# From the output projection on: three engines in source order, the squares of the norm later, FFN sums in accumulators

## The chip, the core and the metric

The kernel runs on one core of one Trainium2 chip. The metric is device time in microseconds (us) for one execution. TensorE multiplies matrices into PSUM banks, VectorE and ScalarE work on tiles in SBUF and read PSUM, GpSimd works on SBUF alone, and SyncE's queue issues nearly all transfers. In the rows PE is TensorE's matmuls, PEld its weight loads, DVE VectorE, ACT ScalarE, POOL GpSimd and SP (SPq) SyncE's queue.

## The reference

One layer of a streaming encoder. Two token branches are merged, projected and added to the residual `h`; then comes a feed-forward network and a last norm:

```
def _merge_ffn(h, ya, yb, ga, gb, w_out, norm_ffn, w_up, w_down):
    m = jax.nn.sigmoid(ga) * ya + jax.nn.sigmoid(gb) * yb
    h = h + jnp.einsum('btd,de->bte', m, w_out)
    u = jnp.einsum('btd,df->btf', _rmsnorm(h, norm_ffn), w_up)
    return h + jnp.einsum('btf,fd->btd', jnp.square(jax.nn.relu(u)), w_down)
```

`w_out` is 1024 x 1024, `w_up` 1024 x 4096, `w_down` 4096 x 1024, all float32. There are 544 columns of tokens (16 meta tokens with padding, 32 of a running stream, 512 of the prompt). Since relu squared of a scaled row is the scale squared times relu squared, the FFN is computed on unnormed `h`, and the norm's factor r2 = 1/(mean of h squared + eps) is multiplied in after the down projection.

## The kernel before, in words

Every float32 matrix is split in two: a rounded high part, made by ScalarE (`split_hi`, a copy), and the remainder, made by VectorE (`split_lo`, a subtraction). A product is three matmuls: high x high, low x high, high x low. All weights are loaded by SyncE into three slots (tag `raw`, 512 KB each), split, and kept in two slots (`whi`, `wlo`).

The stages of interest, in order:

- **Output projection** ("wo"), eight units of 48 matmuls in the order `WO_ORDER`. `evac_o` (VectorE) adds the result into `xr`, which becomes `hs[d]`, the residual. `operands(d)` then makes of two such tiles, d and d + 4, the seven combined operands (B11, BM, B21, B22, BT4, BN, BT3) that the next stage multiplies, each split in `hh` and `hl`. GpSimd squares `hs[d]` and sums the squares into `sqa`.
- Four **chunks** (`ch`), each an up stage and a down stage. The **up stage** has four pairs (`up_pair`); a pair is a Strassen-like scheme of seven products of 12 matmuls: first a11 and s1, then s2, s4, s3, a12, a22. They go into three PSUM banks, X, V and Y. The first, third, fifth and seventh product all add into X, and between them ScalarE copies X out (L1327, L1333, L1340, L1350), so that each of these products must wait for the copy that comes before it. Then relu squared (L1345, L1351; VectorE), `uh` (ScalarE) and `ul` (VectorE), first for two of four quarters, then for the other two.
- The **down stage** has eight units d of 48 matmuls; VectorE multiplies each result by r2 into `dt` (L1396), and GpSimd (VectorE in the last chunk) adds it to `hs[d]` (L1398). In the last chunk transposes, the last norm and the output follow in between (`final_part`, `final_norm`).

Weights of a pair are prepared in steps by the generator `pair_prep`: s31 (two sums at once, L280), s24 (L285, L288), and the splits. Its four loads fill two `raw` tiles: u2 (a21 and a12) and u1 (a11 and a22). The steps of pair p + 1 are written between the products of pair p: `pre(1)` runs one step of the generator that was started last. `use(key)` finishes a unit's steps and starts the loads of the next one. u2's slot comes free with the split of a12, u1's with that of a22.

What sets the order: the kernel's text is not the order in which engines run it. A planner goes through all instructions when the kernel is built, with costs of its own, and gives each engine its instructions in the order in which it finds them ready. Each engine then works down its list, waiting on semaphores. So in the trace before, steps of `pair_prep` stand earlier or later than in the text, as it fitted.

Of the kernel before, what the change touches and what calls it, by code (L numbers as in the profile page):

```python
# [8 lines left out]
F32 = mybir.dt.float32  # L9
# [6 lines left out]
P = 128  # L16
# [31 lines left out]
def tile_hybrid_step(  # L48
# [13 lines left out]
    tpool = ctx.enter_context(tc.tile_pool(name="tpool", bufs=1))  # L62

# [192 lines left out]
    def pair_prep(n, key, parts):  # L256
# [920 lines left out]


# [7 lines left out]
    sqa = pairw["R"].tile([P, TM], F32, name="sqa")  # L1186
# [7 lines left out]
    def operands(d):  # L1194
        j, g = d % 4, gffn[:, d: d + 1]
        H_, L_ = hH[j], hL[j]

        def split(i, src):
            n = src.shape[1]
            split_hi(H_[:, i: i + n, :], src)  # L1200
            split_lo(L_[:, i: i + n, :], src, H_[:, i: i + n, :])

        if d < 4:
            bt = bts[0] = pairw["R"].tile([P, 3, HT], F32, tag="bt", name=f"bt{j}")
            ACT.activation(bt[:, 0:3:2, :], halves(hs[d]), AF.Copy, scale=g)
            DVE.tensor_tensor(bt[:, 1, :], bt[:, 0, :], bt[:, 2, :], ALU.subtract)
            split(B11, bt[:, 0:2, :])
# [7 lines left out]
        split(BN, bt[:, 1:3, :])
        split(B21, b2)
        DVE.scalar_tensor_tensor(bt[:, 0, :], bt[:, 1, :], -1.0, b2[:, 0, :], ALU.mult, ALU.subtract)
        split(BT4, bt[:, 0:1, :])

    bts = [None]  # L1220
    for n, d in enumerate(WO_ORDER):
# [3 lines left out]
        if n == KD - 1:  # L1225
            pre(3)
# [21 lines left out]
    pre(3)  # L1248

# [68 lines left out]
    def up_pair(ch, j):  # L1318
# [4 lines left out]
        u = fpool.tile([P, 4, HT], F32, tag="u", name=f"u{ch}_{j}", bufs=2)  # L1323
# [17 lines left out]
        DVE.tensor_tensor(u[:, 3, :], x3, u[:, 3, :], ALU.add)  # L1341
        pre(1)
        product(Y, W["a12"], B21, True)
        DVE.tensor_tensor(u[:, 0, :], yv, u[:, 0, :], ALU.add)
        DVE.scalar_tensor_tensor(u[:, 0:2, :], u[:, 0:2, :], 0.0, u[:, 0:2, :], ALU.max, ALU.mult)  # L1345
        split_hi(uh[:, 0:2, :], u[:, 0:2, :])
        split_lo(ul[:, 0:2, :], u[:, 0:2, :], uh[:, 0:2, :])
        pre(1)
        product(X, W["a22"], BT4, False)
        ACT.activation(u[:, 2, :], xv, AF.Copy)  # L1350
        DVE.scalar_tensor_tensor(u[:, 2:4, :], u[:, 2:4, :], 0.0, u[:, 2:4, :], ALU.min, ALU.mult)  # L1351
        split_hi(uh[:, 2:4, :], u[:, 2:4, :])
        split_lo(ul[:, 2:4, :], u[:, 2:4, :], uh[:, 2:4, :])
        pre(1)
# [6 lines left out]
    for ch in range(NCH):  # L1361
        uh, ul = [], []
        for j in range(4):
            h_, l_ = up_pair(ch, j)
            uh.append(h_)
            ul.append(l_)
            if ch == 0 and j == 1:
                for a, b in OC:
                    ps = psany(f"ps_r2_{a}")
                    mm(ps[:, : b - a], ones_d, sqa[:, a:b], True, True)  # L1370
                    DVE.tensor_scalar(r2[:, a:b], ps[:, : b - a], EPS, None, ALU.add)
                    DVE.reciprocal(r2[:, a:b], r2[:, a:b])
        last_ch = ch == NCH - 1
        for d in range(KD):
# [13 lines left out]
            for ci, part in (((0, 0), (1, 0), (0, 1), (1, 1)) if d == 0 else ((0, 0), (0, 1), (1, 0), (1, 1))):  # L1388
# [52 lines left out]
```

## Time and profile before

| | us |
|---|---|
| median of the runs | 837.34 |
| lowest run | 835.44 |
| the profiled execution, its own time | 835.72 |
| span of its trace | 834.0 |
| TensorE matmuls busy | 805.4 (97%) |
| VectorE busy | 561.7 (67%) |
| ScalarE busy | 355.6 (43%) |
| GpSimd busy | 192.3 (23%) |

The mean granted clock of TensorE was 0.989 of full speed. A busy share is a mean over all stages; the stages have different limits, so it is the rows by stage that tell what sets the time. In a timeline row the last bracket gives how long the engine had sat idle and what released it.

### The profile page before, as it was taken

To read this page: it belongs to the slowest core of one execution; us is meant where nothing else is said; L and a number is where in the kernel's file an instruction comes from. 1 tells how busy PE (TensorE), PEld (TensorE's weight loads), DVE (VectorE), ACT (ScalarE), POOL (GpSimd) and SP (SyncE) were. 2 spreads that over 40 slices of the span, in tenths; PEclk is the share of its full clock that TensorE was granted. 3 is DMA by queue.
4 is the path that set the end of the run, shared out by engine and by line. 5 is a ranking of instruction groups with operands and counts; after the bars stand their busy time and mean duration, and the time that the engine had idled before them with its cause. 6 is when DMAs were issued, how large, how long until landed. Compare 5 with 4: busy or idle time off the path is not lost.

```text
span 834.0 us, 15007 instructions
## 1 busy us (share of the span) xinstructions
PE 805.4 (97%) x6087; PEld 771.7 (93%) x6087; DVE 561.7 (67%) x1020; ACT 355.6 (43%) x663; POOL 192.3 (23%) x194
## 2 busy tenths in 40 slices
PE   8998999999999999999997999999999999999995
PEld 6877898898999999999996999999999999999995
DVE  5866258798768464467679893689438873688554
ACT  6761454555445632322444641246214551255223
POOL 4315112211121384015445002210122002300000
PEclk8999999999999999999998999999999999999999
DMA  8523223431521123232223342332332332414202
GB/s 246 153 59 90 51 54 94 124 78 51 134 80 51 51 76 103 76 101 77 85 68 102 84 119 76 85 94 79 104 97 77 101 102 85 118 52 129 75 26 108
DMA packets 133303, 75.38 MB, mean 90 GB/s; under 512 B 14545, under 2 KB 128513, under 8 KB 133233
## 3 DMA queue, kind: packets, MB, share of 16 engines
q1 hardware_dynamic: 132192, 72.27, 30.8%
q0 software_dynamic: 1024, 2.14, 1.1%
q8 instruction: 48, 0.79, 0.4%
q14 instruction: 23, 0.18, 0.1%
q10 hardware_dynamic: 16, 0.00, 0.0%
HBM read 69.57 MB, written 4.83 MB: 89 GB/s over the span
## 4 chain that ended last, share of the span: by engine, by line
PE 67%; DVE 15%; DMA 7%; ACT 5%; POOL 3%; issue 3%; SPq 0%; ACTq 0%; POOLq 0%; DVEq 0%
PE ps_dn L117 23%; PE ps_gb L117 5%; PE ps_ga L117 5%; PE ps_x L117 5%; DMA wr<-in_w_up_dram 4%; PE ps_fv L117 3%; PE ps_ya L117 3%; PE ps_yb L117 3%; PE ps_fk L117 2%; PE ps_v L117 2%; PE ps_wo L117 2%; DVE wlo L123 2%; DVE wl L123 2%; PE ps_y L117 2%; DMA wr<-in_w_in_dram 2%
## 5 line engine op out<-in xcount | busy, mean ns | idle before, releaser
L120 ACT ACTIVATE wh<-wr 128x1024 fp32r<-128x1024 f32 x78 | 82.4, 1057 | 184.4 <-PE ps_dn L117 82.7
L123 DVE TENSOR_TENSOR wl<-wr,wh 128x1024 fp32r<-128x1024 f32 x78 | 113.5, 1456 | 31.3 <-ACT wh L120 30.8
L1398 POOL TENSOR_TENSOR xres<-xres,dt 128x288 f32<-128x288 f32 (+1 forms) x48 | 41.2, 864 | 235.1 <-DVE dt L1396 235.1
L245 POOL TENSOR_TENSOR wr<-wr,gmix 128x1024 f32<-128x1024 f32 x30 | 58.1, 1938 | 144.8 <-DMA wr<-in_w_in_dram 111.2
L117 PE MATMUL ps_dn<-uh,wl 128*128 128x256 f32 (+1 forms) x512 | 85.6, 288 | 0.0
L117 PE MATMUL ps_dn<-ul,wh 128*128 128x256 f32 (+1 forms) x512 | 85.2, 288 | 0.0
L117 PE MATMUL ps_dn<-uh,wh 128*128 128x256 f32 (+1 forms) x512 | 85.0, 288 | 0.0
L117 PEld LDWEIGHTS ps_dn<-ul,wh 128*128 128x128 f32 x512 | 72.6, 189 | 0.0
L117 PEld LDWEIGHTS ps_dn<-uh,wl 128*128 128x128 f32 x512 | 72.5, 188 | 0.0
L117 PEld LDWEIGHTS ps_dn<-uh,wh 128*128 128x128 f32 x512 | 72.3, 188 | 0.0
L1396 DVE TENSOR_TENSOR dt<-ps_dn,fin 128x288 f32<-128x288 f32 x64 | 28.0, 439 | 65.5 <-PE ps_dn L117 65.3
L120 ACT ACTIVATE whi<-s 128x512 fp32r<-128x512 f32 (+1 forms) x32 | 27.0, 842 | 37.7 <-issue 14.4
L117 PE MATMUL ps_x<-hh,whi 128*128 128x272 f32 x128 | 37.9, 296 | 3.6 <-ACT hh L120 1.9
L117 PE MATMUL ps_x<-hh,wlo 128*128 128x272 f32 x128 | 37.8, 295 | 1.0 <-DVE wlo L123 0.9
L117 PE MATMUL ps_x<-hl,whi 128*128 128x272 f32 x128 | 37.5, 293 | 0.6 <-DVE hl L123 0.6
L117 PE MATMUL ps_v<-hh,whi 128*128 128x272 f32 x128 | 37.8, 296 | 0.1
L117 PE MATMUL ps_v<-hl,whi 128*128 128x272 f32 x128 | 37.5, 293 | 0.0
L117 PE MATMUL ps_v<-hh,wlo 128*128 128x272 f32 x128 | 37.3, 292 | 0.0
L123 DVE TENSOR_TENSOR wlo<-s,whi 128x512 fp32r<-128x512 f32 (+1 forms) x32 | 33.9, 1060 | 4.7 <-ACT whi L120 4.7
L907 ACT ACTIVATE sb<-sb,m 128x144 f32<-128x144 f32 (+3 forms) x32 | 18.3, 573 | 36.3 <-DVE m L902 36.3
L280 DVE TENSOR_TENSOR s<-wr,wr 128x1024 f32<-128x1024 f32 x16 | 20.0, 1252 | 16.7 <-DMA wr<-in_w_up_dram 16.7
L120 ACT ACTIVATE uh<-u 128x544 fp32r<-128x544 f32 x32 | 21.0, 658 | 21.9 <-DVE u L1351 11.2
(463 smaller groups left out, 2231.3 us busy)
## 6 DMA issues: line engine op xcount, KB each, us to landing
wr<-in_w_up_dram SPq DMA_DIRECT2D x64, 256.0 KB, 3.4
wr<-in_w_down_dram SPq DMA_DIRECT2D x32, 512.0 KB, 4.1
wr<-in_w_in_dram SPq DMA_DIRECT2D x30, 512.0 KB, 3.9
wr<-in_w_out_dram SPq DMA_DIRECT2D x8, 512.0 KB, 3.9
cb<-cPd SPq DMA_DIRECT2D x8, 264.0 KB, 3.9
x_t<-in_x_prompt_dram SPq DMA_DIRECT2D x4, 512.0 KB, 5.4
gvraw<-in_w_in_dram SPq DMA_DIRECT2D x4, 512.0 KB, 8.2
fvraw<-in_w_in_dram SPq DMA_DIRECT2D x4, 512.0 KB, 3.9
```

What stands on the lines that cost most here:

```text
L117: return TE.matmul(out, lhsT, rhs, start=start, stop=stop, skip_group_check=True)
L120: ACT.activation(out, in_, AF.Copy)
L123: (eng or DVE).tensor_tensor(out, in_, hi.bitcast(F32), ALU.subtract)
L245: POOL.tensor_tensor(raw, raw, gmix.unsqueeze(2).to_broadcast([P, KD, P]), ALU.mult)
L280: DVE.tensor_tensor(s31, u1, u2[:, 0:1].to_broadcast([P, 2, k4, P]), ALU.add)
L907: exps.append(ACT.activation(sb, sb, AF.Exp, bias=m, scale=-1.0, accum_out=rs).ins)
L1396: DVE.tensor_tensor(dt_[:, : b - a], ps[:, : b - a], r2[:, a:b], ALU.mult)
L1398: (DVE if last_ch else POOL).tensor_tensor(hs[d][:, a:b], hs[d][:, a:b], dt_[:, : b - a], ALU.add)
```

## The change

Three things change. First, from the line where the output projection begins, TensorE, ScalarE and VectorE no longer get a planned order: they take their instructions in the order of the source. GpSimd and SyncE stay planned. The source is rearranged along with it: steps of `pair_prep` and of `operands` are reordered, a step stands ahead of the copy that follows a product, and the seven quarters' tiles become pairs of halves (`half_pair`). Second, the squares of `hs[d]` and their sum move from the output projection to the down stage of chunk 0, and r2 to the first unit of chunk 1's down stage. Third, the down results of chunks 0 to 2 are gathered unscaled in `acc[d]` (ScalarE copies in chunk 0, VectorE adds in chunks 1 and 2); after chunk 2 VectorE multiplies by r2 and adds to `hs[d]`. GpSimd's 48 additions are gone.

```
+    vpool = ctx.enter_context(tc.tile_pool(name="vpool", bufs=1))
...
         if key[0] == "dn":
-            yield
+            for _ in range(4 if key[2] == 0 else 1):
+                yield
...
         s31 = t(pairw["R"], "s31", 2, F32)
         DVE.tensor_tensor(s31, u1, u2[:, 0:1].to_broadcast([P, 2, k4, P]), ALU.add)
-        A = t(wpool, "whi", bufs=2), t(wpool, "wlo", bufs=2)
-        split(A, 0, ["a11"], u1[:, 0:1])
         yield
         s24 = t(pairw["R"], "s24", 2, F32)
         DVE.tensor_tensor(s24[:, 0], s31[:, 1], u1[:, 0], ALU.add)
+        yield
+        A = t(wpool, "whi", bufs=2), t(wpool, "wlo", bufs=2)
+        split(A, 0, ["a11"], u1[:, 0:1])
+        DVE.tensor_tensor(s24[:, 1], s24[:, 0], u2[:, 1], ALU.add)
+        yield
         split(A, 1, ["s1"], s31[:, 1:2])
         yield
-        DVE.tensor_tensor(s24[:, 1], s24[:, 0], u2[:, 1], ALU.add)
         B = t(wpool, "whi", bufs=2), t(wpool, "wlo", bufs=2)
-        yield
         split(B, 0, ["s2", "s4"], s24)
         yield
...
+        for nm, src in (("s3", s31[:, 0:1]), ("a12", u2[:, 1:2]), ("a22", u1[:, 1:2])):
+            split((t(pairw["L"], nm + "h", 1), t(pairw["L"], nm + "l", 1)), 0, [nm], src)
+            yield
...
+    ordered = ctx.enter_context(tc.manual_schedule(
+        engines={mybir.EngineType.PE, mybir.EngineType.Activation, mybir.EngineType.DVE}))
...
+    def operands(d, mid=None):
...
         ACT.activation(b2, halves(hs[d]), AF.Copy, scale=g)
+        DVE.scalar_tensor_tensor(bb[:, 0, :], ba[:, 1, :], -1.0, b2[:, 1, :], ALU.mult, ALU.subtract)
+        DVE.tensor_tensor(bb[:, 1, :], b2[:, 1, :], bb[:, 1, :], ALU.subtract)
+        if mid:
+            mid()
+        hi(BN, bb)
+        hi(B21, b2)
+        DVE.scalar_tensor_tensor(ba[:, 0, :], bb[:, 0, :], -1.0, b2[:, 0, :], ALU.mult, ALU.subtract)
+        lo(BN, bb)
+        hi(BT4, ba[:, 0:1, :])
+        lo(B21, b2)
+        lo(BT4, ba[:, 0:1, :])
...
         if n == KD - 1:
-            pre(3)
+            pre(4)
...
-            POOL.tensor_tensor(sqa, xr, xr, ALU.mult)
-            POOL.tensor_tensor(sq, xr, xr, ALU.mult)
-            POOL.tensor_tensor(sqa, sqa, sq, ALU.add)
+        operands(d, (lambda: pre(1)) if n == KD - 1 else None)
...
     def up_pair(ch, j):
...
         product(X, W["a11"], B11, True)
+        pre(1)
+        ACT.activation(fa[:, 0, :], xv, AF.Copy)
         product(V, W["s1"], BM, True)
+        pre(1)
+        ACT.activation(fb[:, 1, :], vv, AF.Copy)
         product(X, W["s2"], BN, False)
+        pre(1)
+        ACT.activation(fa[:, 1, :], xv, AF.Copy)
         product(V, W["s4"], B22, False)
+        pre(1)
+        DVE.tensor_tensor(fa[:, 1, :], vv, fa[:, 1, :], ALU.add)
         product(X, W["s3"], BT3, False)
+        pre(1)
         x3 = fpool.tile([P, HT], F32, tag="x3", name=f"x3_{ch}_{j}", bufs=2)
         ACT.activation(x3, xv, AF.Copy)
+        DVE.tensor_tensor(fb[:, 1, :], x3, fb[:, 1, :], ALU.add)
         product(Y, W["a12"], B21, True)
         pre(1)
+        DVE.tensor_tensor(fa[:, 0, :], yv, fa[:, 0, :], ALU.add)
+        DVE.scalar_tensor_tensor(fa, fa, 0.0, fa, ALU.max, ALU.mult)
         product(X, W["a22"], BT4, False)
+        split_hi(uh[:, 0:2, :], fa)
         pre(1)
+        split_lo(ul[:, 0:2, :], fa, uh[:, 0:2, :])
+        ACT.activation(fb[:, 0, :], xv, AF.Copy)
+        DVE.scalar_tensor_tensor(fb, fb, 0.0, fb, ALU.min, ALU.mult)
+        split_hi(uh[:, 2:4, :], fb)
+        split_lo(ul[:, 2:4, :], fb, uh[:, 2:4, :])
...
                 if not part:
                     continue
+                if ch == 0:
+                    if ci == 0:
+                        acc[d] = blk([TM], F32, f"acc{d}", "v")
+                    ACT.activation(acc[d][:, a:b], ps[:, : b - a], AF.Copy)
+                    continue
+                if not last_ch:
+                    DVE.tensor_tensor(acc[d][:, a:b], ps[:, : b - a], acc[d][:, a:b], ALU.add)
+                    if ch == NCH - 2:
+                        DVE.tensor_tensor(acc[d][:, a:b], acc[d][:, a:b], r2[:, a:b], ALU.mult)
+                        DVE.tensor_tensor(hs[d][:, a:b], acc[d][:, a:b], hs[d][:, a:b], ALU.add)
+                    continue
...
+            if ch == 0:
+                sq = blk([TM], F32, f"hsq{d}", "v")
+                POOL.tensor_tensor(sq, hs[d], hs[d], ALU.mult)
...
+            if ch == 1 and d == 0:
+                for a, b in OC:
...
+                    DVE.reciprocal(r2[:, a:b], r2[:, a:b])
```

Here `fa` and `fb` hold quarters 0 and 1, and 2 and 3, of what was the tile `u`. `mid` is the split of s2 and s4 for the first pair. The loop over `OC` that makes r2 stood behind pair 1 of chunk 0 before. The work of TensorE, and VectorE's and ScalarE's work in the up stages, stays the same in number and size.

## Rows read from the trace of the kernel before

**Rows 1.** Windows: stretch, length, busy us (instructions) of PE, PEld, DVE, ACT, POOL; clock, DMA.

```profile
392.80:443.00 50.20, 48.85 (x385) 48.18 (x385) 35.83 (x53) 21.82 (x31) 23.60 (x15) 1.00 0.27 77
443.00:496.70 53.70, 48.09 (x344) 45.89 (x343) 49.87 (x74) 28.26 (x52) 10.40 (x5) 0.94 0.34 98
496.70:545.00 48.30, 48.30 (x387) 48.30 (x386) 24.10 (x33) 10.77 (x14) 11.93 (x14) 1.00 0.34 96
```

**Rows 2.** The same view, columns as in rows 1, chunk 0's first pair.

```profile
449.00:452.00 3.00, 1.62 (x8) 1.42 (x8) 3.00 (x3) 1.49 (x3) 2.92 (x3) 0.86 0.02 5
452.00:455.00 3.00, 1.46 (x6) 1.14 (x6) 3.00 (x4) 1.51 (x4) 1.71 (x2) 0.50 0.14 55
455.00:458.00 3.00, 3.00 (x16) 3.00 (x15) 2.87 (x6) 1.18 (x3) 0.00 (x0) 0.51 0.32 120
```

**Rows 3.** The chain of waits: start, length, engine, tile, line, instructions.

```profile
458.40 1.51 PE ps_x L117 x12
...
496.74 48.29 PE ps_dn L117 x384
...
588.45 48.27 PE ps_dn L117 x384
...
680.32 48.27 PE ps_dn L117 x384
...
771.47 24.14 PE ps_dn L117 x192
```

**Rows 4.** Timeline of VectorE and GpSimd, last operands before chunk 0.

```profile
449.59 2.07 POOL L1239 TENSOR_TENSOR hsq<-xres 128x544 f32<-128x544 f32 x1
...
450.63 1.32 DVE L1213 SCALAR_TENSOR_TENSOR bt<-bt,b 128x272 f32<-128x272 f32 x1
```

**Rows 5.** Groups of VectorE's instructions in chunk 1's up stage, count | busy, mean ns.

```profile
L280 DVE TENSOR_TENSOR s<-wr,wr 128x1024 f32<-128x1024 f32 x3 | 3.7, 1221 | 1.3 <-DMA wr<-in_w_up_dram 1.3
...
L1341 DVE TENSOR_TENSOR u<-x,u 128x272 f32<-128x272 f32 x4 | 1.7, 434 | 0.0
```

**Rows 6.** The same groups for ScalarE, chunk 1's up stage.

```profile
L120 ACT ACTIVATE whi<-s 128x1024 fp32r<-128x1024 f32 x4 | 4.2, 1058 | 6.4 <-issue 4.6 <-PE ps_v L117 1.2 <-DVE s L288 0.6
...
L120 ACT ACTIVATE ch<-s 128x512 fp32r<-128x512 f32 x3 | 1.9, 626 | 2.0 <-PE ps_y L117 2.0
```

**Rows 7.** Timeline of ScalarE, chunk 1's up stage, into its second pair.

```profile
545.10 1.06 ACT L120 ACTIVATE whi<-s 128x1024 fp32r<-128x1024 f32 x1 [4.60 <-issue]
...
557.52 0.40 ACT L1327 ACTIVATE u<-ps_x 128x272 f32<-128x272 f32 x1 [0.32 <-PE ps_x L117]
558.81 0.66 ACT L120 ACTIVATE uh<-u 128x544 fp32r<-128x544 f32 x1 [0.89 <-DVE u L1351]
559.38 0.38 ACT L1330 ACTIVATE u<-ps_v 128x272 f32<-128x272 f32 x1
```

**Rows 8.** Timeline of VectorE over the same pairs.

```profile
555.62 0.68 DVE L123 TENSOR_TENSOR cl<-s,ch 128x512 fp32r<-128x512 f32 x1
556.23 0.68 DVE L123 TENSOR_TENSOR cl<-wr,ch 128x512 fp32r<-128x512 f32 x1
...
558.07 0.72 DVE L1351 SCALAR_TENSOR_TENSOR u<-u 128x544 f32<-128x544 f32 x1
559.51 0.73 DVE L123 TENSOR_TENSOR ul<-u,uh 128x544 fp32r<-128x544 f32 x1 [0.72 <-ACT uh L120]
...
561.21 1.22 DVE L280 TENSOR_TENSOR s<-wr,wr 128x1024 f32<-128x1024 f32 x1
```

**Rows 9.** Timeline of SyncE's queue over the same pairs.

```profile
556.94 2.15 SPq L264 DMA_DIRECT2D wr<-in_w_up_dram  x4
```

**Rows 10.** The instructions of line 1250: ns min/median/max, first and last start.

```profile
L1250 ACT ACT_TABLE_LOAD  x1: 1283/1283/1283, 347.0 to 347.0; - x1
```

**Rows 11.** Timeline of VectorE, end of the last down stage.

```profile
824.10 0.42 DVE L1396 TENSOR_TENSOR dt<-ps_dn,fin 128x256 f32<-128x256 f32 x1
...
824.61 1.40 DVE L1304 TENSOR_SCALAR ytok<-ytok,r3r 32x600 f32<-32x600 f32 x3
```

More of the change, by code (lines that the diff above doesn't have):

```diff
@@ L1192, in halves, with half_pair, hi, lo @@
         return v.rearrange("p (s t) -> p s t", s=2)
-    def operands(d):
+    def half_pair(name):
+        return pairw["R"].tile([P, 2, HT], F32, tag="ur", name=name, bufs=4)
+    def operands(d, mid=None):
         j, g = d % 4, gffn[:, d: d + 1]
         H_, L_ = hH[j], hL[j]
[L1198 to L1201, printed above, removed]
+        def hi(i, src):
+            split_hi(H_[:, i: i + src.shape[1], :], src)
+        def lo(i, src):
+            split_lo(L_[:, i: i + src.shape[1], :], src, H_[:, i: i + src.shape[1], :])
@@ L1203, in operands @@
         if d < 4:
[L1204 to L1207, printed above, removed]
+            ba, bb = bts[0] = half_pair(f"ba{j}"), half_pair(f"bb{j}")
+            ACT.activation(ba[:, 0, :], hs[d][:, 0:HT], AF.Copy, scale=g)
+            ACT.activation(bb[:, 1, :], hs[d][:, HT:], AF.Copy, scale=g)
@@ L1208, in operands @@
+            DVE.tensor_tensor(ba[:, 1, :], ba[:, 0, :], bb[:, 1, :], ALU.subtract)
+            hi(B11, ba)
+            lo(B11, ba)
             return
-        bt = bts[0]
-        b2 = pairw["R"].tile([P, 2, HT], F32, tag="b2", name=f"b2{j}")
+        ba, bb = bts[0]
+        b2 = half_pair(f"b2{j}")
         ACT.activation(b2, halves(hs[d]), AF.Copy, scale=g)
-        DVE.scalar_tensor_tensor(bt[:, 1, :], bt[:, 1, :], -1.0, b2[:, 1, :], ALU.mult, ALU.subtract)
-        DVE.tensor_tensor(bt[:, 2, :], b2[:, 1, :], bt[:, 2, :], ALU.subtract)
@@ L1215, in operands @@
[L1215 to L1218, printed above, removed]
+        DVE.scalar_tensor_tensor(bb[:, 0, :], ba[:, 1, :], -1.0, b2[:, 1, :], ALU.mult, ALU.subtract)
[5 more added lines that the diff above has]
+        DVE.scalar_tensor_tensor(ba[:, 0, :], bb[:, 0, :], -1.0, b2[:, 0, :], ALU.mult, ALU.subtract)
@@ L1248, in tile_hybrid_step @@
     pre(3)
+    acc = [None] * KD
     act_set = ACT.preload_act_table_set("natural_log_exp_and_others")
@@ L1322, in up_pair @@
         ul = upool.tile([P, 4, HT], F32R, tag="ul", name=f"ul{ch}_{j}")
[L1323 removed]
+        fa, fb = half_pair(f"fa{ch}_{j}"), half_pair(f"fb{ch}_{j}")
         X, V, Y = [psany(f"ps_{x}{ch}_{j}") for x in "xvy"]
@@ L1326, in up_pair @@
         product(X, W["a11"], B11, True)
-        ACT.activation(u[:, 0, :], xv, AF.Copy)
         pre(1)
+        ACT.activation(fa[:, 0, :], xv, AF.Copy)
         product(V, W["s1"], BM, True)
-        ACT.activation(u[:, 3, :], vv, AF.Copy)
         pre(1)
+        ACT.activation(fb[:, 1, :], vv, AF.Copy)
         product(X, W["s2"], BN, False)
-        ACT.activation(u[:, 1, :], xv, AF.Copy)
         pre(1)
+        ACT.activation(fa[:, 1, :], xv, AF.Copy)
         product(V, W["s4"], B22, False)
-        DVE.tensor_tensor(u[:, 1, :], vv, u[:, 1, :], ALU.add)
         pre(1)
+        DVE.tensor_tensor(fa[:, 1, :], vv, fa[:, 1, :], ALU.add)
         product(X, W["s3"], BT3, False)
+        pre(1)
         x3 = fpool.tile([P, HT], F32, tag="x3", name=f"x3_{ch}_{j}", bufs=2)
         ACT.activation(x3, xv, AF.Copy)
-        DVE.tensor_tensor(u[:, 3, :], x3, u[:, 3, :], ALU.add)
+        DVE.tensor_tensor(fb[:, 1, :], x3, fb[:, 1, :], ALU.add)
+        product(Y, W["a12"], B21, True)
         pre(1)
[L1343 to L1347, printed above, removed]
-        pre(1)
[L1349 to L1354, printed above, removed]
+        DVE.tensor_tensor(fa[:, 0, :], yv, fa[:, 0, :], ALU.add)
+        DVE.scalar_tensor_tensor(fa, fa, 0.0, fa, ALU.max, ALU.mult)
+        product(X, W["a22"], BT4, False)
+        split_hi(uh[:, 0:2, :], fa)
+        pre(1)
+        split_lo(ul[:, 0:2, :], fa, uh[:, 0:2, :])
[3 more added lines that the diff above has]
+        split_lo(ul[:, 2:4, :], fb, uh[:, 2:4, :])
         return uh, ul
@@ L1366, in tile_hybrid_step @@
             ul.append(l_)
[L1367 to L1372, printed above, removed]
         last_ch = ch == NCH - 1
@@ L1394, in tile_hybrid_step @@
                     continue
-                dt_ = fpool.tile([P, CUT - M0], F32, tag="dt", name=f"dt{ch}_{d}_{ci}", bufs=4)
+                if ch == 0:
[9 more added lines that the diff above has]
+                    continue
+                dt_ = fpool.tile([P, CUT - M0], F32, tag="dt", name=f"dt{ch}_{d}_{ci}", bufs=3)
                 DVE.tensor_tensor(dt_[:, : b - a], ps[:, : b - a], r2[:, a:b], ALU.mult)
-                if not last_ch or d < 7 or ci == 0:
-                    (DVE if last_ch else POOL).tensor_tensor(hs[d][:, a:b], hs[d][:, a:b], dt_[:, : b - a], ALU.add)
-                if last_ch and d == 7:
+                if d < 7 or ci == 0:
+                    DVE.tensor_tensor(hs[d][:, a:b], hs[d][:, a:b], dt_[:, : b - a], ALU.add)
+                if d == 7:
                     tiles = ((0, 1, 2), (3, 4))[ci]
@@ L1402, in tile_hybrid_step @@
                     final_norm(tiles[0], tiles[-1] + 1)
+            if ch == 0:
+                sq = blk([TM], F32, f"hsq{d}", "v")
+                POOL.tensor_tensor(sq, hs[d], hs[d], ALU.mult)
+                if d == 0:
+                    sqa = sq
+                else:
+                    POOL.tensor_tensor(sqa, sqa, sq, ALU.add)
+            if ch == 1 and d == 0:
+                for a, b in OC:
+                    ps = psany(f"ps_r2_{a}")
+                    mm(ps[:, : b - a], ones_d, sqa[:, a:b], True, True)
+                    DVE.tensor_scalar(r2[:, a:b], ps[:, : b - a], EPS, None, ALU.add)
+                    DVE.reciprocal(r2[:, a:b], r2[:, a:b])
             if last_ch and d == 3:
```

14 lines of the change are left out of this document (1 added, 13 removed).

## The prediction, made before the changed kernel had run

> **What bounds the kernel now.** I read the windows by stage first: before the output projection nothing changes, so only what follows counts. A down stage is full of matmuls, 48.30 us busy of 48.30, while VectorE works 24.1 and GpSimd 11.9 of them: nothing can be won there, and there is room beside [rows 1]. The output projection leaves TensorE 1.35 us idle of 50.2, and chunk 0's up stage 5.6 of 53.7, part of it at a granted clock of half [rows 1, 2]. The chain of waits gives the other up stages: from the end of one block of down matmuls to the start of the next, 545.03 to 588.45, 636.72 to 680.32 and 728.59 to 771.47, which is 43.42, 43.60 and 42.88 [rows 3]. A product of 12 matmuls takes 1.51 [rows 3], so 28 of them need 42.3, and 0.6 to 1.3 is lost in each.
>
> The one large loss is where the output projection hands over. It ends at 443.02, and the fourth product ends at 458.40 [rows 3]: 15.4 for 6.0 of work. VectorE is full there and slowed by GpSimd's squares: next to a square of 2.07, L1213 took 1.32 [rows 4], an instruction of the size that takes 0.43 elsewhere [rows 5]. So the most that the change can win is some 9 there, 0.6 in the projection (one wait for a weight's remainder that the squares had slowed) and 0.6 to 1.3 in each of three up stages: about 13.
>
> **The change, up stages of chunks 1 to 3.** TensorE waits little there because the planner has moved work around; VectorE is nearly as full as TensorE. Per pair VectorE has, in both kernels, two instructions of 1024 columns (1.22), seven of 512 (0.68), three of 272 (0.43) and four of 544 (0.72) [rows 5, 8]. The next one starts 0.07 to 0.08 before the last has ended (555.62 to 556.23 for 0.68 [rows 8]), so a pair takes 2 x 1.14 + 7 x 0.60 + 3 x 0.35 + 4 x 0.64 = 10.1 of TensorE's 7 x 1.51 = 10.6. Half a microsecond is left for waits. I now go down VectorE's list in source order, with 0.04 from one engine's end to the other's start (559.47 to 559.51 [rows 7, 8]):
> - After L1351 it has only `ul`, which needs `uh` from ScalarE: idle 0.72 as in [rows 8], and no overlap, 0.8 in all. Before, this happened in some pairs; now in each.
> - After L1345 comes the remainder of a12. Its high part stands on ScalarE behind `uh`, and `uh` needs L1345: 0.04 + 0.56 + 0.63 + 0.04 [rows 6, 7], with the overlap 1.3. Before, a12 was split ahead of `uh` [rows 8].
> - s2 and s4: ScalarE needs 1.06 [rows 6], VectorE has 0.95 to do meanwhile: 0.3.
> - Two instructions that need the one just before them: 0.1 each.
> - s31 of the pair after next needs u1, whose slot comes free with a12. Before, a12 ended at 556.91, the load was issued at 556.94 [rows 8, 9] and s31 could start by 561.21 [rows 8]. I take 3.6 for this; VectorE has 3.2 to do meanwhile: 0.4.
>
> Sum 3.0, so VectorE needs 13.1 for a pair, 2.6 more than TensorE. That reaches TensorE through ScalarE: the third product writes bank X, so it waits for the copy L1327, and in the source this copy stands behind `uh` of the pair before (which needs L1351) and behind the split of a22. Before, the copy ran at 557.52, ahead of `uh` at 558.81 [rows 7]. So when L1351 starts later than about 0.8 into a pair, TensorE waits; before it started at 558.07 [rows 8], 2.5 into its pair, and nothing depended on it.
>
> Walking the lists of a stage: in the last down unit s2 and s4 need the weight slot of that unit, so their split starts at its end (545.10 against 545.03 [rows 3, 7]); before, a12 was split long before that, now it stands behind it in both lists. It is done 3.5 into the up stage, u1 of the second pair has landed at 7.1, and ScalarE holds that pair's s1 and s2/s4 ahead of copies that the first pair's products need: 0.3 + 1.3 + 1.1 of waits. The second pair waits 3.2 at its third product; the third and fourth 2.6 each, the difference of the rounds. Together 11.1, so a stage takes 42.3 + 11.1 = 53.4, against 43.42, 43.60 and 42.88: **+30.3** for the three. In the fourth pair only a down weight is prepared (1.22), so VectorE has caught up when the down stage begins.
>
> **Chunk 0's up stage.** The first two products now find their operands ready, and GpSimd's squares are gone: the 9.3 as they stand in the trace are gone. But other waits come in their place. VectorE finishes the operands of the last unit but one 3.5 after that unit's end, 2.5 before the last unit's, and then has five instructions of `pre(4)` (1.14 + 4 x 0.6 + 0.1) and two additions before the last residual is complete: 1.9 after the projection's end. From there ScalarE must do in order, before the third product may start: the copy b2, s2/s4, BN, B21, a wait of 0.5 for VectorE, BT4, s3, a12, a22, the table load of 1.28, which before ran under other work at 347.0 [rows 10], and only then the first copy. With the durations of [rows 6, 7], each less 0.1 of overlap: 1.9 + 0.64 + 0.96 + 2 x 0.56 + 0.5 + 0.33 + 3 x 0.53 + 1.28 + 0.4 = 8.7. The product was due at 3.0, so it waits 5.7. Then 0.3 and 1.1 in this pair, 3.2, 2.6 and 2.6 in the others as above: 42.3 + 15.5 = 57.8. Before it was 496.74 - 443.02 = 53.7 [rows 3], r2's four matmuls among it, which now lie in chunk 1 and cost there what they cost here. I take 0.8 for them, an estimate: four matmuls of up to 288 columns at twice the 0.13 of one of 272 (1.51 / 12 [rows 3]), less what runs beside them. Without them it is 52.9: **+4.9**. In 449 to 458 the granted clock fell to 0.50 with TensorE 1.62 and 1.46 of 3 busy [rows 2]; a wait of 5.7 is emptier, so I let it fall again. Those nine microseconds lost 3.4 of full clock, which bounds the price from 0 to 3.4; VectorE sets the pace behind it and hides part: I take **1.8**.
>
> **The rest.** Projection: the wait of 0.6 for a remainder slowed by a square goes: **-0.6**. Squares and sums, 15 GpSimd instructions, under chunk 0's down stage: VectorE's one remainder per unit (1.22 of 6.03) has the rest of the unit as cover, so 0; without that cover it would be some 0.9 per unit, as beside L1213 [rows 1, 4, 5]. `acc`: ScalarE's copies have the same cover, VectorE's additions replace the multiplications, 0 as long as a down stage is TensorE's. GpSimd's additions held nobody: 0. The end: in source order the last `dt` (824.10 before) stands behind the scaling that began at 824.61 [rows 11] and ran 1.3; ScalarE has its own share of that scaling until shortly after, so I take **+0.7** of a bound from 0 to 1.9.
>
> Sum: +30.3 + 4.9 + 1.8 - 0.6 + 0.7 = +37 on the profiled execution's 835.7, which is 1.6 below the median of 837.34 and as near to the lowest run: **873** (VectorE's round is the likeliest case).
>
> **Rivals.**
> - *A: VectorE keeps step.* If L1351 ends early enough that the copy is done by the third product, in the up stages nothing is lost and the handover's gain stays: -9 - 0.6 + 0.7, **827**. It decides at a wait of about 0.7 per pair (12 pairs with a predecessor, gain 9): below it the change is no loss. For it: the handover's losses are real [rows 2, 4]. Against: 10.1 of 10.6 is taken before any wait, and two of the waits follow from three neighbouring source lines. An order of the source that binds less than it says would give the same time. 0.14.
> - *B: half the lag.* VectorE holds the timetable of before, only ScalarE's order costs: `uh` ended at 559.47 [rows 7], the copy 0.4 later, the third product was due at about 558.5: 1.4 per pair, 12 times, less the gain of 9: **843**; with the first pairs' waits, up to 856. 0.16.
> - *C: the clock falls at the waits.* Each wait of 2.6 or 3.2 costs a stretch at 1.2 GHz as in [rows 2]. Each stretch would add up to 3.4, hidden in part since the next wait shrinks; I get 4.4 per stage by doubling the products that follow a long wait: 3 x 4.4 = 13, **886**. Against: TensorE would be 80% busy per pair, against half in [rows 2]. The Trainium skill, "TensorE: Matmul & The Clock Gate", section "HAM oscillation — how this bites in real kernels", tells of a kernel whose clock fell anew in each turn of its loop because of the wait in it; by that, this rival holds. The trace shows such a fall for one place only. 0.12.
> - The forecast itself, 857 to 882: 0.58.
>
> **How the numbers follow.** A measurement of this kernel can tell about 2% from no change, 820.6 to 854. Faster by more needs 16.7, above the 13 that can be had: 0.02. Within: A and most of B, 0.25. Slower: 0.73. The range leaves out A and the outer end of C: 843 to 889. The loads' time is the least certain term: with 4.4 for u1 in place of 3.6 the walk gives 2.5 more per stage, 883, which lies within.
>
> **What will show it.** Right: an idle TensorE of 2 to 3 us once per pair at the third product, released by ScalarE's L1327 copy of X; VectorE with 0.7 to 1.4 idle, released by ScalarE's splits, at two places in each pair; up stages of 53; the down stages still 48.3; the first pair of chunk 0 with one long wait behind ScalarE; no GpSimd beside the handover. Wrong: up stages of 43 to 45 (A), `uh` behind the copy of the next pair, or half clock in the up stages (C). The weakest step is that VectorE's waits add up over a pair and are not eaten by TensorE's own delay.

## The result, and the profile after

The changed kernel takes 899.37 us (median of 4 runs, 889.94 to 900.45) against 839.86 for the kernel before: ratio 1.0685, 95% interval 1.0645 to 1.0724, slower by 6.9%. One of the four runs behind the 839.86 took 1560.02 us and the ratio leaves it out, so it is not the quotient of the two medians. The prediction had 873, 843 to 889. The direction holds, the size does not. The profiled execution took 898.32, its span 896.6.

The windows by stage, columns as in [rows 1]: the projection, chunk 0's up and down stages, the up stages of chunks 1 to 3.

```profile
397.10:446.46 49.36, 48.62 (x386) 48.18 (x385) 31.19 (x54) 21.80 (x34) 5.39 (x5) 1.00 0.27 78
446.46:515.95 69.49, 47.83 (x338) 46.48 (x337) 54.54 (x67) 28.66 (x54) 22.03 (x16) 0.88 0.26 76
515.95:564.23 48.28, 48.28 (x386) 48.28 (x385) 14.38 (x15) 15.20 (x27) 0.00 (x0) 1.00 0.27 78
564.23:621.95 57.72, 46.95 (x339) 45.62 (x337) 38.12 (x57) 25.30 (x50) 0.00 (x0) 0.94 0.29 83
...
671.14:727.92 56.78, 46.90 (x338) 45.57 (x337) 38.43 (x58) 25.14 (x49) 0.00 (x0) 0.94 0.29 84
...
776.20:833.20 57.00, 46.89 (x338) 45.55 (x337) 39.84 (x62) 25.12 (x49) 0.00 (x0) 0.94 0.29 84
```

Four things stand in these rows. The up stages of chunks 1 to 3 went from 43.42, 43.60 and 42.88 [rows 3] to 57; chunk 0's from 53.7 [rows 1] to 69.5. GpSimd is busy 22.0 us in chunk 0's up stage and not at all in its down stage, where the squares were meant to lie: they did not move there. And the granted clock is below 1 in every up stage, 0.94 in those of chunks 1 to 3. The down stages are full, as before.

The list of waits of TensorE, over the whole run (engine, tile, line, released by: us in total, times, longest):

```profile
PE ps_x L118 <- ACT fa L1337: 40.1, 14, 9.6
PE ps_x L118 <- ACT fa L1343: 6.9, 4, 2.3
PE ps_x L118 <- ACT x L1350: 4.0, 3, 1.3
```

The first line is the predicted one: ScalarE's first copy of bank X (now line 1337), for which each pair's third product waits. The longest is at the handover, 9.65 where 5.7 was predicted. GpSimd's and VectorE's timelines say why (start, length, instruction, idle time before it):

```profile
446.30 0.61 POOL L1263 DMA_DIRECT2D fin<-in_norm_final_dram  x1 [43.97 <-PE ps_wo L118]
446.92 2.15 POOL L1419 TENSOR_TENSOR hsq<-xres 128x544 f32<-128x544 f32 x2
...
450.81 1.09 POOL L1419 TENSOR_TENSOR hsq<-xres 128x544 f32<-128x544 f32 x1
451.98 1.41 POOL L1423 TENSOR_TENSOR hsq<-hsq,hsq 128x544 f32<-128x544 f32 x1
...
467.79 1.33 POOL L1423 TENSOR_TENSOR hsq<-hsq,hsq 128x544 f32<-128x544 f32 x1
```

```profile
451.15 1.05 DVE L1222 SCALAR_TENSOR_TENSOR bb<-ba,b 128x272 f32<-128x272 f32 x1 [0.82 <-ACT b L1221]
452.12 1.56 DVE L1223 TENSOR_TENSOR bb<-b,bb 128x272 f32<-128x272 f32 x1
453.61 2.11 DVE L124 TENSOR_TENSOR wlo<-s,whi 128x1024 fp32r<-128x1024 f32 x1
...
458.65 1.85 DVE L124 TENSOR_TENSOR hl<-b,hh 128x544 fp32r<-128x544 f32 x1
```

The source writes the squares in the down loop, but only TensorE, ScalarE and VectorE were put in source order. GpSimd's list was left to the planner, the squares' inputs were ready, and so they ran right behind GpSimd's load issue at the end of the projection, 446.92 to 469.1, next to the handover. VectorE's instructions of 272 columns take 1.05 and 1.56 there, for 1.32 beside a square before [rows 4] and 0.43 elsewhere [rows 5].

In the steady pairs VectorE's timeline is the predicted one (chunk 1, from one pair's s31, line 283, to the next):

```profile
572.88 1.23 DVE L283 TENSOR_TENSOR s<-wr,wr 128x1024 f32<-128x1024 f32 x1 [4.28 <-DMA wr<-in_w_up_dram]
...
577.24 1.23 DVE L124 TENSOR_TENSOR wlo<-s,whi 128x1024 fp32r<-128x1024 f32 x1 [0.25 <-ACT whi L121]
...
581.78 0.69 DVE L124 TENSOR_TENSOR a12l<-wr,a12h 128x512 fp32r<-128x512 f32 x1 [1.25 <-ACT a12h L121]
...
584.47 0.72 DVE L124 TENSOR_TENSOR ul<-fb,uh 128x544 fp32r<-128x544 f32 x1 [0.72 <-ACT uh L121]
...
586.41 1.23 DVE L283 TENSOR_TENSOR s<-wr,wr 128x1024 f32<-128x1024 f32 x1 [0.62 <-DMA wr<-in_w_up_dram]
```

From s31 to s31 is 13.53, predicted 13.1, where TensorE needs 10.6. Windows of 3 us show the clock, in chunk 0's and in chunk 2's up stage:

```profile
455.00:458.00 3.00, 0.00 (x0) 0.00 (x0) 3.00 (x3) 0.77 (x2) 3.00 (x2) 0.50 0.00 0
...
470.00:473.00 3.00, 3.00 (x15) 3.00 (x14) 2.97 (x6) 1.40 (x2) 0.00 (x0) 0.50 0.06 17
...
692.00:695.00 3.00, 3.00 (x16) 3.00 (x15) 2.50 (x4) 1.06 (x3) 0.00 (x0) 0.50 0.59 175
...
719.00:722.00 3.00, 3.00 (x15) 3.00 (x15) 0.26 (x1) 0.32 (x2) 0.00 (x0) 0.50 0.49 142
```

Some 15 or 16 matmuls run in 3 us at 0.50 (1.2 GHz), where some 24 run at 2.4 GHz (12 take 1.51 [rows 3]). The first lies in the handover's wait, the second behind a wait of 2.33 at the fifth product. In chunks 1 to 3 each of the six stretches follows a wait of 2.6 to 2.9 at a third product: the one at 692 a wait of 2.94 that ended at 691.3.

### The profile page after: what moved, and what is told of

It reads as the page before. It is cut to its first block, busy times and chain, and to the rows that moved or that the text cites. A ratio compares the mean times of both kernels' runs of the same rounds, so it can differ in the third digit from the quotient of the medians.

```text
span 896.6 us, 14940 instructions
## 1 busy us (share of the span) xinstructions
PE 822.9 (92%) x6087; PEld 786.8 (88%) x6087; DVE 568.0 (63%) x1036; ACT 360.2 (40%) x683; POOL 144.4 (16%) x146
## 4 chain that ended last, share of the span: by engine, by line
PE 63%; DVE 17%; ACT 8%; DMA 5%; issue 4%; POOL 3%; SPq 0%; ACTq 0%; DVEq 0%; POOLq 0%
PE ps_dn L118 21%; PE ps_x L118 6%; PE ps_gb L118 5%; PE ps_ga L118 5%; PE ps_wo L118 3%; PE ps_fv L118 3%; PE ps_ya L118 3%; PE ps_yb L118 2%; DMA wr<-in_w_up_dram 2%; DVE wlo L124 2%; PE ps_v L118 2%; PE ps_fk L118 2%; ACT whi L121 2%; DVE wl L124 1%; DMA wr<-in_w_in_dram 1%
## 5 line engine op out<-in xcount | busy, mean ns | idle before, releaser
L124 DVE TENSOR_TENSOR wl<-wr,wh 128x1024 fp32r<-128x1024 f32 x78 | 107.7, 1381 | 63.1 <-ACT wh L121 62.3
L118 PE MATMUL ps_x<-hh,whi 128*128 128x272 f32 x128 | 41.2, 322 | 40.1 <-ACT fa L1337 40.1
L118 PEld LDWEIGHTS ps_x<-hh,whi 128*128 128x128 f32 x128 | 26.3, 205 | 43.7 <-ACT fa L1337 43.7
L118 PE MATMUL ps_v<-hh,wlo 128*128 128x272 f32 x128 | 39.6, 309 | 1.4 <-DVE wlo L124 1.4
L118 PE MATMUL ps_x<-hl,whi 128*128 128x272 f32 x128 | 40.0, 313 | 0.0
L118 PE MATMUL ps_v<-hh,whi 128*128 128x272 f32 x128 | 39.7, 310 | 0.0
L118 PE MATMUL ps_x<-hh,wlo 128*128 128x272 f32 x128 | 39.6, 309 | 0.0
L1404 DVE TENSOR_TENSOR acc<-ps_dn,acc 128x288 f32<-128x288 f32 (+1 forms) x32 | 14.1, 439 | 30.3 <-PE ps_dn L118 30.2
L118 PEld LDWEIGHTS ps_v<-hh,wlo 128*128 128x128 f32 x128 | 26.9, 210 | 1.6 <-DVE wlo L124 1.6
```

The costliest lines, as they stand in the source:

```text
L118: return TE.matmul(out, lhsT, rhs, start=start, stop=stop, skip_group_check=True)
L124: (eng or DVE).tensor_tensor(out, in_, hi.bitcast(F32), ALU.subtract)
L1404: DVE.tensor_tensor(acc[d][:, a:b], ps[:, : b - a], acc[d][:, a:b], ALU.add)
```

## The experiments

The stages of all kernels, from the first matmul of one stage to that of the next, in us, and each kernel's ratio to the kernel before, measured beside it (so the row of the kernel before has several medians):

| kernel | up 0 | up 1 | up 2 | up 3 | median | ratio, 95% interval |
|---|---|---|---|---|---|---|
| before | 53.4 | 43.4 | 43.6 | 42.9 | 835.04 to 840.94 | |
| the change | 69.5 | 57.7 | 56.8 | 57.0 | 899.37 | 1.0685 (1.0645 to 1.0724) |
| e1 planner's order | 59.0 | 43.1 | 43.1 | 44.2 | 845.29 | 1.0059 (1.0028 to 1.0089) |
| e2 source order alone | 70.0 | 61.1 | 61.0 | 61.0 | 914.76 | 1.0885 (1.0833 to 1.0936) |
| e3 squares held back | 62.0 | 55.4 | 55.9 | 54.9 | 888.08 | 1.0571 (1.0527 to 1.0615) |
| e4 both e1 and e3 | 46.0 | 43.5 | 43.1 | 44.4 | 832.51 | 0.9914 (0.9884 to 0.9944) |
| e5 one more product | 69.3 | 54.4 | 54.6 | 54.9 | 890.32 | 1.0624 (1.0577 to 1.0671) |
| e6 e3, steps earlier | 55.1 | 51.4 | 50.6 | 50.8 | 863.85 | 1.0316 (1.0277 to 1.0354) |
| e7 e3, tail behind two copies | 63.1 | 60.8 | 61.1 | 61.0 | 902.37 | 1.0766 (1.0718 to 1.0814) |
| e8 e6 and e7 | 59.5 | 57.0 | 57.0 | 54.6 | 886.20 | 1.0577 (1.0536 to 1.0619) |
| e9 e3, tail behind one copy | 57.4 | 54.0 | 55.0 | 56.3 | 875.35 | 1.0466 (1.0407 to 1.0525) |
| e10 e6 and e9 | 54.0 | 50.5 | 49.5 | 50.0 | 864.56 | 1.0320 (1.0270 to 1.0370) |

The theory after the result: the order costs the time, by the round of VectorE and ScalarE, by the clock at the waits, and by squares that stayed at the handover. The rivals: the new work itself costs it; the one copy that TensorE waits for costs it; the clock is only a symptom.

**e1 and e2, everything but the order, and the order alone.** e1 leaves out

```
-    ordered = ctx.enter_context(tc.manual_schedule(
-        engines={mybir.EngineType.PE, mybir.EngineType.Activation, mybir.EngineType.DVE}))
```

and e2 adds these two lines, alone, to the kernel before.

> The changed kernel with the line that puts TensorE, ScalarE and VectorE in source order left out, so that the planner orders them as in the kernel before; the squares, the accumulators, the half tiles and the new operand order stay. Theory (the source order costs the time: VectorE's round of 13.5 us a pair, TensorE waiting in order behind it, and the clock that falls at those waits): the up stages of chunks 1 to 3 come back from 57 to 43 to 45 us each; the squares still run on GpSimd right behind the projection, so the first up stage keeps some of its excess, between 54 and 62; 838 to 850 in all. Rival (the new work itself costs it: accumulators, half tiles, moved squares): the up stages stay above 50 and the time above 870.

> The kernel before with nothing but the line that puts the three engines in source order. Theory: its up stages of chunks 1 to 3 take 53 to 60 us each, TensorE waits for VectorE's and ScalarE's results in each pair, granted clock below 1 in these stages; the first up stage, whose squares run under the projection as before, is at 58 to 64, not 69.6; 870 to 900 in all. Rival (the new work costs it): within 10 us of before. A second rival, that the order of the new steps (operand parts, weight parts) is what makes source order slow: up stages clearly under 50.

e1's up stages of chunks 1 to 3 are back at 43 to 44, its clock at 1.00 there: accumulators, half tiles and the new steps cost nothing in them. The first up stage is 59.0, longer than before, with GpSimd busy 24.56 us beside it:

```profile
442.80:501.80 59.00, 49.29 (x338) 47.68 (x337) 55.19 (x66) 27.57 (x51) 24.56 (x16) 0.86 0.30 89
550.10:593.20 43.10, 42.53 (x338) 42.31 (x337) 34.86 (x53) 25.51 (x47) 0.00 (x0) 1.00 0.30 87
```

e2 makes the kernel slower by more than the whole change does: what else the change does, its new order of steps among it, wins back some 4 us in each stage. The numbers expected for e2 were too low, though: 61 us per stage for 53 to 60, 914.76 in all for 870 to 900, and a first up stage of 70.0 for 58 to 64. Of GpSimd's work only the last unit's square and sum run near its handover. Its VectorE alternates with ScalarE there (idle 0.82, 0.72, 0.49 and 0.50 before operands and remainders, each released by ScalarE), and its third product waits 9.40. So a long handover alone does not prove the squares guilty; that needs e3.

**e3 and e4, squares that really lie under the down stage.** e3 is the changed kernel with one line more, which makes a square wait for its block's accumulator; e4 is e1 with it.

```
+                POOL.tensor_copy(sq[:, 0:1], acc[d][:, 0:1])
                 POOL.tensor_tensor(sq, hs[d], hs[d], ALU.mult)
```

> The changed kernel, with a copy of one column of each chunk-0 accumulator into the tile of that block's square ahead of the square, so that GpSimd can't start a square before the accumulator is there: the squares then really lie under the first down stage. Same result. Theory (the squares beside the handover stretch VectorE's instructions and with them the wait for the third product): the first up stage falls from 69.6 to 57 to 62 us, the third product's wait from 9.65 to 4.5 to 6.5, the first down stage grows by at most 2; 885 to 892 in all. Rival (the squares do no harm there, the first pair is long by its order alone): first up stage 66 to 70, time 896 to 901.

> Both at once: the planner's order for the three engines, and the squares held behind the accumulators. Theory: nothing is left of what cost time, the up stages of chunks 1 to 3 at 43 to 44 us, the first at 48 to 53 (before: 53.7), the time 828 to 838, at or under the kernel before. Rival (accumulators and half tiles cost by themselves, through buffers or ScalarE's copies): over 845.

As the theory has it. e3's windows of the four up stages, then the same VectorE instructions as above, and the third product:

```profile
447.66:509.62 61.96, 49.62 (x339) 48.73 (x338) 42.80 (x67) 28.67 (x53) 0.52 (x1) 0.86 0.29 85
557.96:613.32 55.36, 43.87 (x338) 42.54 (x337) 38.06 (x57) 25.32 (x50) 0.78 (x1) 1.00 0.30 86
662.51:718.40 55.89, 46.70 (x338) 45.36 (x337) 38.40 (x58) 25.16 (x49) 0.00 (x0) 0.94 0.30 85
766.70:821.64 54.94, 43.90 (x339) 42.56 (x338) 39.72 (x62) 25.14 (x49) 0.00 (x0) 1.00 0.30 86
```

```profile
450.19 0.44 DVE L1222 SCALAR_TENSOR_TENSOR bb<-ba,b 128x272 f32<-128x272 f32 x1 [0.82 <-ACT b L1221]
450.54 0.43 DVE L1223 TENSOR_TENSOR bb<-b,bb 128x272 f32<-128x272 f32 x1
...
453.26 0.72 DVE L124 TENSOR_TENSOR hl<-b,hh 128x544 fp32r<-128x544 f32 x1
```

```profile
456.50 0.59 PE L118 MATMUL ps_x<-hh,whi 128*128 128x272 f32 x1 [5.58 <-ACT fa L1337]
```

L1223 is 0.43 for 1.56, the third product waits 5.58 (predicted 5.7) for 9.65, and the first up stage is 7.5 shorter. The Trainium skill, "SBUF — State Buffer", section "Who interferes with whom", says that a VectorE instruction with both inputs in SBUF contends with a GpSimd instruction that reads SBUF, and that the ports they share are an exclusive lock. The change's rows agree to 0.14: L1222 began at 451.15 beside a square that ended at 451.90, L1223 at 452.12 beside a sum that ended at 453.39. What was left of the neighbour and their own 0.44 and 0.43 make 1.19 and 1.70; measured are 1.05 and 1.56.

e4's first up stage is 46.0, for 48 to 53 expected, and e4 is the best kernel of the study, 0.9% under the kernel before (0.6 to 1.2%, by the interval):

```profile
447.30:493.30 46.00, 43.28 (x338) 42.45 (x337) 40.98 (x65) 27.26 (x51) 0.41 (x1) 1.00 0.38 112
541.60:585.10 43.50, 42.80 (x339) 42.36 (x338) 35.99 (x55) 25.54 (x47) 0.88 (x1) 1.00 0.34 95
```

**e5, the clock.** One product more in each pair of the changed kernel, in the place where TensorE waits:

```
+        product(Y, W["a11"], B11, True)
         product(X, W["s2"], BN, False)
```

> The changed kernel with one more product in each pair, 12 matmuls ahead of the third product (the first product's operands once more, into the bank that the sixth product starts afresh): TensorE works 1.5 us of the wait that it had there. Same result. Theory (the falls of the clock at the waits cost 1 to 2 us of each up stage, by the stages with and without a fall in the runs so far): the granted clock stays at 1 in most of the up stages of chunks 1 to 3 and they take 55 us, as the undisturbed ones of the gated kernel, not 57; 890 to 895 in all. Rival (the falls cost nothing, the round of VectorE and ScalarE alone sets the pair): 57 us whatever the clock, 896 to 901. Second rival (a pair is bound by TensorE's own work plus its waits): each pair 1.5 us longer, stages of 63, 918.

The up stages of chunks 1 to 3 keep full clock and take 54.4, 54.6 and 54.9, for 57.7, 56.8 and 57.0: with 12 matmuls more per pair, 2.5 less per stage. Chunk 1's:

```profile
558.30:612.70 54.40, 49.51 (x386) 48.48 (x385) 38.08 (x57) 25.24 (x50) 0.00 (x0) 1.00 0.30 88
```

So the falls cost time, and the rival, that the pair's round runs on whatever the clock, is refuted. What a fall costs hangs on where it stands: two of them give TensorE some 3 us more of busy time per stage (46.9 for 43.9 in the windows of the change and of e3). Behind a fall in the second pair, the wait of the third pair's third product is shorter, here in chunk 1 of the change and of e3, whose clock stays at 1.00:

```profile
599.26 0.39 PE L118 MATMUL ps_x<-hh,whi 128*128 128x272 f32 x1 [1.61 <-ACT fa L1337]
```

```profile
592.12 0.39 PE L118 MATMUL ps_x<-hh,whi 128*128 128x272 f32 x1 [2.66 <-ACT fa L1337]
```

The change's second fall stands in the fourth pair, where no next wait takes it up. In e3's chunk 2 both falls stand in pairs with a successor, and that stage, 55.9, is only 0.5 to 1.0 longer than its neighbours, where the change's stages are 1.4 to 2.8 longer than those. This is read from the rows; no run moves a fall alone. In chunk 0, where the wait stays at 8.2, the clock still fell and the stage stayed at 69.3. The time itself, 0.6% lower by the two ratios, has intervals that overlap; the stages carry this conclusion.

**e6 to e10, which part of the order.** e6 moves two weight steps ahead (`pre` runs one step of the next pair's weights): the a12 step ahead of the first half's `uh`, the a22 step ahead of the second half's.

```
+        pre(1)
         split_hi(uh[:, 0:2, :], fa)
-        pre(1)
         split_lo(ul[:, 0:2, :], fa, uh[:, 0:2, :])
         ACT.activation(fb[:, 0, :], xv, AF.Copy)
         DVE.scalar_tensor_tensor(fb, fb, 0.0, fb, ALU.min, ALU.mult)
+        pre(1)
         split_hi(uh[:, 2:4, :], fb)
```

e9 makes the pair's last four instructions a function, run in the next pair behind its first copy and ahead of the step with s31 (the fourth pair of a chunk runs it at once). e7 has the two `tails` lines behind the copy of V instead, the first `pre` left in its place. e8 is e6 with e7, e10 is e6 with e9.

```
-        pre(1)
         ACT.activation(fa[:, 0, :], xv, AF.Copy)
+        if tails:
+            tails.pop()()
+        pre(1)
         product(V, W["s1"], BM, True)
...
+        def tail():
+            ACT.activation(fb[:, 0, :], xv, AF.Copy)
+            DVE.scalar_tensor_tensor(fb, fb, 0.0, fb, ALU.min, ALU.mult)
+            split_hi(uh[:, 2:4, :], fb)
+            split_lo(ul[:, 2:4, :], fb, uh[:, 2:4, :])
...
```

> The gated kernel with two steps of the next pair's weights earlier in the source, so that VectorE and ScalarE have them in the gaps: the a12 step ahead of the first half's uh, the a22 step ahead of the second half's uh. Nothing is added or taken away. Theory (VectorE's round in source order sets the pair: 13.5 us, of which 1.24 it waits for a12h behind uh and 0.72 for uh): the round falls to 11.3 to 12, the up stages of chunks 1 to 3 from 55 to 47 to 51, the time to 862 to 875. Rival (the round is set by TensorE's wait for the copy of X on ScalarE, behind the previous pair's uh and a22h): uh of the second half is no earlier, the stages stay at 53 to 56, 880 to 888.

> The gated kernel with the last four instructions of a pair (copy of X, square of the second half, its uh and ul) moved in the source behind the next pair's first two copies, for the first three pairs of a chunk: the copy for which TensorE waits 2.7 us a pair no longer stands behind uh. Theory (VectorE's round sets the pair): TensorE's wait for that copy goes, but 1.24 for a12h stays in VectorE's round, which falls only to 12.3 to 13, and TensorE waits elsewhere in the pair; up stages of chunks 1 to 3 at 50 to 54, 872 to 884. Rival (that copy is the cause): 2.7 us less for each of three pairs, stages at 46 to 48, 858 to 866.

> Both edits on the gated kernel: the a12 and a22 steps earlier, and the pair's last four instructions behind the next pair's copies. Theory: VectorE's round near its busy time of 10.5 to 11.3, about TensorE's 10.6, up stages of chunks 1 to 3 at 44 to 48, the first at 50 to 56, 838 to 858: source order can be written to nearly what the planner gives (832.5), and does not beat it. Rival (source order as such costs, by the loads or by queues that no order mends): stages above 50, over 865.

e6 came out at the upper end of what the theory says: stages of 50.6 to 51.4 for 47 to 51, a round of 12.1 for 11.3 to 12. Its VectorE no longer shows the 1.25 and 0.72, but waits 0.94 for the load:

```profile
569.12 1.23 DVE L283 TENSOR_TENSOR s<-wr,wr 128x1024 f32<-128x1024 f32 x1 [0.99 <-DMA wr<-in_w_up_dram]
...
581.23 1.23 DVE L283 TENSOR_TENSOR s<-wr,wr 128x1024 f32<-128x1024 f32 x1 [0.94 <-DMA wr<-in_w_up_dram]
```

e7 fits neither theory, with 61 per stage. e8, with 54.6 to 57.0 and 886.20, misses the theory's 44 to 48 and lies where its rival put it: above 50, over 865, by loads or queues that no order mends. VectorE's timeline in e7:

```profile
580.17 1.23 DVE L283 TENSOR_TENSOR s<-wr,wr 128x1024 f32<-128x1024 f32 x1 [2.74 <-DMA wr<-in_w_up_dram]
...
582.04 0.72 DVE L1367 SCALAR_TENSOR_TENSOR fb<-fb 128x544 f32<-128x544 f32 x1
...
597.13 1.23 DVE L283 TENSOR_TENSOR s<-wr,wr 128x1024 f32<-128x1024 f32 x1 [2.67 <-DMA wr<-in_w_up_dram]
```

The moved square (line 1367 there) had come to stand behind s31, which waits 2.7 for a load; and ScalarE's `uh`, which needs the square, stands ahead of the copy for the fifth product, which waited 4.71. The round became 17.0. My expectation had missed what the moved instructions were queued behind. e9 and e10 put them ahead of s31.

> The gated kernel with the pair's last four instructions behind the next pair's first copy alone, and ahead of the step whose s31 waits for a load (behind the second copy they stood behind that wait: 2.7 us at each pair on VectorE). Theory (the round of VectorE and ScalarE sets the pair; what stands in source order behind a wait pays it): TensorE's wait for the first copy goes, VectorE's round loses the 0.6 it waited for the load but not the 1.24 for a12h, so 12.7 to 13.2 a pair, up stages of chunks 1 to 3 at 52 to 54.5, 876 to 886; the waits of TensorE stand at other products. Rival (the copy behind uh is what costs): stages at 46 to 48, 858 to 866. Second rival (deferring the tail costs by itself, load or no load): stages at 57 or more, as when it stood behind the second copy.

> The same, with the a12 and a22 steps earlier as well. Theory: round 11.4 to 12 (12.1 where the steps alone were earlier, of which 0.94 waited for the load that now has more time), up stages of chunks 1 to 3 at 47.5 to 50.5, 852 to 863. Rival (the load of the next pair's quarters limits the round, not the order of the instructions): VectorE's wait for it stays at 0.9 or more and the stages at 50.5 to 52.

e9 tells the two theories apart. TensorE's wait for the first copy fell from 2.7 to 0.26, yet VectorE's round stayed:

```profile
568.30 1.23 DVE L283 TENSOR_TENSOR s<-wr,wr 128x1024 f32<-128x1024 f32 x1 [0.67 <-DMA wr<-in_w_up_dram]
...
577.18 0.69 DVE L124 TENSOR_TENSOR a12l<-wr,a12h 128x512 fp32r<-128x512 f32 x1 [1.25 <-ACT a12h L121]
...
581.85 1.23 DVE L283 TENSOR_TENSOR s<-wr,wr 128x1024 f32<-128x1024 f32 x1 [0.66 <-DMA wr<-in_w_up_dram]
```

13.55 as before, stages of 54.0 to 56.3 for 54.9 to 55.9 in e3, and the waits stand at other products (1.0 behind the copy of V, 0.9 behind that of X after the fifth product). The biggest line in the list of waits was thus not the cause. The theory's own numbers were too low here, a round of 12.7 to 13.2 and stages of 52 to 54.5: the 0.66 for the load stayed. e9's time, 875, lies under the range given although its stages do not: its first up stage has one fall of the clock where e3's has three (57.4 for 62.0), and the code before the projection, the same in both, took 7 us less in its profile. e10's stages are 49.5 to 50.5, as expected; its time of 864.56 is not below e6's, and just over the 852 to 863 given. The load's wait fell to 0.3 to 0.4, but 0.72 for `uh` came back, and the round is 12.1 as in e6. e10's stages are 4.6 to 7.5 us shorter than e8's, whose last instructions stand behind the load; but no source order that was tried came under 49.5 in chunks 1 to 3, where the planner's has 43 to 44. Whether one can is not shown.

## Why the prediction was wrong

**The direction and the main mechanism held.** VectorE's round in source order is longer than TensorE's, and that is most of what the change costs: e1 against the change, e6 and e9 show it. The waits stand where the text put them: 1.25 for a12 (1.3 with the overlap), 0.72 for `uh` (0.8), 0.25 for s2/s4 (0.3). The end, +0.7, came out: from the start of the last down stage to the span's end it is 62.5 before [rows 3] and 63.2 after (833.37 to 896.6). So did the projection (-0.9 for -0.6) and the 0.8 for r2's four matmuls (chunk 1's down stage is 49.2 for 48.3). One slip is small: 13.1 less 10.6 is 2.5 a pair, not 2.6.

The profile, 898.3, is 25.3 over the 873. Four terms make it up.

- **"GpSimd's squares are gone" from the handover: the step that failed.** I costed the squares under chunk 0's down stage at 0 because the source writes them there, and never asked which engines are in source order. The diff names three, and GpSimd is not one of them. The text even listed "no GpSimd beside the handover" as a sign. What the runs show in its place: the planner put all 15 of these instructions beside the handover, 446.92 to 469.1. Cost: 7.5 (e3 against the change, 62.0 for 69.5). With the squares really moved, the handover's wait was 5.58 for 5.7, and the time was 888.08 (e3).
- **The clock in the pairs, put at nothing: the second step that failed.** Rival C, put at 0.12, happened in part: every up stage has falls. Against it I had argued that TensorE would be 80% busy per pair; it was, and the clock fell all the same. Its price was 2.5 per stage (e5), where C had 4.4, so 6 to 7.5 of the excess. In chunk 0, 2.4 more are left (62.0 in e3 for 57.8 + 1.8). I put them down to the falls behind the second and later waits, which 1.8 did not cover: e9, with the same first wait and one fall for three, takes 57.4, but no run tests this, or the 1.8, alone.
- **The load of u1: mis-sized.** I took 3.6 from the end of a12 to s31. Measured: 582.47 to 586.41, 3.94, in a steady pair, and 568.00 to 572.88, 4.88, in the first. The text had named this the least certain term, with 2.5 per stage for 4.4. e3's two stages at full clock, 55.4 and 54.9, are 1.75 over the 53.4 on average: some 5 for three stages. That these are the load's is argued: its 1.3 and twice 0.3 beyond 3.6 would make 1.9 per stage.
- **Before the projection**, in code that is the same, the profile lost 4.2: the projection starts at 397.1, before at 392.9. In the ten experiments it starts between 391.3 and 399.5, and the mean clock of the first 100 us goes with it: 1.00 in e9 (391.3), 0.97 in the kernel before, 0.95 in the change, 0.91 in e10 (399.5). It is no part of the change.

7.5 + 2.4 + 11.3 (load and clock in three stages: 171.5 less 3 x 53.4) + 4.2 less 0.2 for the projection and the moved sum of squares is 25.2. With the sentence of the Trainium skill in the prediction, by which the clock falls anew in each turn of a loop with a wait in it, the traces agree in kind and not in number: two falls in four pairs in the change's stages, none in two of e3's three with waits of the same length.

What stays open: why the same waits let the clock fall in some stages and not in others, and why the stages at full clock of e5 are 0.5 shorter than e3's.

## What to carry to other kernels

Before costing work as moved, look at which engine runs it, whether that engine's list is in source order, and what data it really waits for: position in the source holds back nothing on an engine that is planned. In an in-order list the longest wait of the bound engine names where the lag comes out, not what makes it; follow the round of the other engines from one pair to the next, and check what a moved instruction is now queued behind, a load above all. What pays is what this change did not do: the planner's order kept, with the squares held back by data (e4, 832.51 us).

## What the runs showed of the hardware

- TensorE with 12 useless matmuls in the wait of each pair finishes the stage 2.5 us sooner (57.2 to 54.6 on average; e5 against the change): its clock stays at 2.4 GHz there.
- The clock fell to 1.2 GHz with TensorE busy some four fifths of a pair, behind waits of 2.0 to 2.9 us (e6's chunk 1 has the shortest, the change's the longest), and did not fall in two of e3's stages with waits of 2.6 to 2.9.
- A GpSimd square next to VectorE costs both: 1.09 alone (e3), up to 1.57 at the handover of the change; the sums 1.36 alone, up to 2.19; VectorE's instructions of 272 columns 1.05 to 1.56 for 0.43.
